# Attention stage of a streaming encoder: key pairs on column halves, one score burst per chunk, and a fixed TensorE order

## The chip, the core and the metric

The kernel is one launch on one core of a Trainium2 chip. The metric is the device time of one execution, in microseconds (us). A core has a tensor engine (PE, with its weight loads shown apart as PEld), a vector engine (DVE), a scalar engine (ACT), GpSimd (POOL) and a sync engine (SP). Each runs its own instruction stream in program order, and a DMA transfer is issued by one of these streams, here by SP and ACT. Matmul results land in PSUM, everything else lives in SBUF.

## The reference

The reference is one inference step of a small hybrid encoder: 2048 prompt tokens and 32 sample tokens, model width 1024. A gated delta-rule layer comes first, then one shared key/value projection, and then the layer that the change is about, sliding-window attention with learned sinks. Its core, shortened:

```python
CHUNK = 64; WINDOW_CHUNKS = 2; B_Q_HEADS = 16; B_KV_HEADS = 4; B_HD = 64

def sink_softmax(s, sinks):
    m = jnp.maximum(s.max(-1, keepdims=True), sinks)
    p = jnp.exp(s - m)
    return p / (p.sum(-1, keepdims=True) + jnp.exp(sinks - m))

# a chunk of 64 queries sees its own 64 keys and those of the two chunks before
s = jnp.einsum('bnqkgd,bnskd->bnkgqs', qb, kb)
o = jnp.einsum('bnkgqs,bnskd->bnqkgd', sink_softmax(s, sinks), vb)
out = (o * jax.nn.silu(z)) @ w_out
y = layer_norm(DN_ALPHA * x + out, ln_g, ln_b)
```

Chunk 0 sees one key chunk and chunk 1 two. The 32 sample tokens attend to 128 cached keys and 32 new ones. All is float32; the big products are done as three passes over a high and a low part of each operand, so that `out` is `g_hi*w_hi + g_hi*w_lo + g_lo*w_hi`.

## The kernel before

The stages run one after the other: projections of the first layer, the delta rule, its output projection and layer norm, then P2 (the query, gate, key and value projections of the second layer), then attention with its output projection. Only the end of P2 and the attention stage are touched.

**P2** (L1279 to L1281) is a list of products, each of 12 matmuls 128x416 in three passes. Its weights come through a ring of 12 tiles `w` of 512 KB, filled by DMAs that ACT issues (L1261). A generator (`late`) hands out the products, so that attention chunks can be set between the last of them.

**Attention** works in chunks of 64 queries, in the order 10 to 31, then 0 to 9. The first four chunks are set between the last P2 products; the rest come after P2. In a chunk there are two head sets (p = 0, 1) of eight heads. For each head set `chunk` does this:

- scores `S` (L1612): matmuls with 64 contraction rows, two of them on the two row halves of the array, into a PSUM tile; there are two `S` tiles after P2 is closed, one before
- softmax: the DVE's `reduce` of `S` for the negated maximum (L1487), a `min` with the sinks into `nm` (L1488), four exponentials on ACT (L1495), `es` (L1496 on DVE, L1497 on ACT), `sm` = sum plus `es` (L1498), its reciprocal (L1499)
- POOL scales the probabilities `P` by `sm` (L1620), in two instructions of 128x384
- six transposes of `P` into PSUM tiles `tr` (L1627), copied to `pt` by ACT (L1629) and by DVE (L1631)
- three value matmuls 128x256 (L1633), one for each key chunk, against `vd`, a block-diagonal 128x128 operand with 64 keys of one head in each diagonal block and zeros elsewhere; `graw` = result times gate, on DVE (L1636)

After two chunks a tile of 128 tokens is complete, and `finish` projects it: the load of `r` (the residual), `g_hi` on ACT (L1508), `g_lo` on POOL (L1509), then two column halves of 512. Each half is 24 matmuls 128x512 (L1520 to L1522) into one PSUM buffer `po`; there is only one such buffer, and the DVE's `r` <- `r`, `po` (L1523, a scalar_tensor_tensor) reads it out before the next half may start. Then come bn_stats (L1524), the layer-norm chain (L1526, POOL L466 and L468, L1530), ACT's scaling of `r` (L1531), and POOL's two passes over the 128x1024 tile, times `ln_g` (L1532) and plus `ln_b` (L1533), and the store of `y`.

The output weights (16 pieces of 512 KB) are loaded on SP after P2's tiles are given back (L999). The order of all engines' instructions in this stage is set by the scheduler of the framework from its own timing model; it puts `po` matmuls of an earlier tile between the steps of a chunk.

## Time and profile before

| what | value |
|---|---|
| median of 3 runs | 2208.47 us (2205.18 to 2213.85) |
| the profiled execution | 2207.43 us |
| its span | 2205.6 us |
| PE busy in the span | 2101.2 us, 95% |
| attention's first scores | 1781.56 us |
| last P2 matmul begins | 1794.63 us |
| last `po` matmul begins | 2195.75 us |

Times in the trace are counted from the start of the span. A timeline row has the start, the duration (both in us), the engine, the line, the operation with out<-in by the program's names, the count, and in brackets how long the engine had been idle and what released it. A group row has the count, the summed busy time and the mean in ns. A windows row has start and end, the length, then busy time and instruction count of PE, PEld, DVE, ACT and POOL, the clock that the tensor engine was granted (1.00 is full), the DMA share and GB/s. A matmul's duration is longer than its pace, since matmuls overlap in the pipeline; the pace is the distance of two starts.

### The profile page before, as it was taken

The page shows a single profiled execution, that of the slowest core. Times are in us where ns is not written, and L with a number is a line of the kernel's source. Part 1 is how long each engine was busy: PE and PEld are TensorE (multiplying, and loading weights), DVE is VectorE, ACT ScalarE, POOL GpSimd, SP SyncE. Part 2 cuts the span into 40 slices and gives each one's busy share as a digit, 9 for nine tenths or more (in the row PEclk, how much of TensorE's full clock was granted, in tenths as well). Part 3 has the DMA queues.
Part 4 walks back from the last instruction along what each step waited for, and adds up shares of the span by engine and source line. Part 5 has one row for each costly group of instructions (what it writes and reads, how often), then busy time and mean ns, then how long its engine had stood idle before and what let it go on. Part 6 is the DMA issues. An engine that isn't in the chain of part 4 may idle for free.

```text
span 2205.6 us, 37189 instructions
## 1 busy us (share of the span) xinstructions
PE 2101.2 (95%) x13370; PEld 1911.0 (87%) x13370; DVE 1486.4 (67%) x2771; ACT 912.1 (41%) x2405; POOL 713.6 (32%) x1176
## 2 busy tenths in 40 slices
PE   8999999999989999998888999899899988999997
PEld 6999999999979899887776888899899976888775
DVE  5889877776557589888865665555835566556663
ACT  5545545544412477677741111311311135444441
POOL 1212211161111288788841210000000025565663
PEclk9999999999999999999999999999999999999999
DMA  7756656567765635436737765888788895333321
GB/s 282 225 185 195 222 168 196 178 192 239 245 213 158 209 130 172 159 124 208 225 108 262 231 205 167 298 280 283 266 278 279 276 301 137 106 87 96 89 79 43
DMA packets 348377, 430.00 MB, mean 195 GB/s; under 512 B 78352, under 2 KB 276080, under 8 KB 348176
## 3 DMA queue, kind: packets, MB, share of 16 engines
q1 hardware_dynamic: 311280, 310.22, 44.3%
q10 hardware_dynamic: 36912, 117.40, 16.0%
q8 instruction: 106, 1.74, 0.3%
q14 instruction: 79, 0.65, 0.1%
HBM read 269.45 MB, written 158.44 MB: 194 GB/s over the span
## 4 chain that ended last, share of the span: by engine, by line
PE 69%; DVE 12%; POOL 5%; DMA 5%; ACT 4%; issue 3%; SPq 1%; ACTq 0%; DVEq 0%; POOLq 0%
PE ps L77 7%; PE ps L79 7%; PE ps L78 7%; PE ps L1279 5%; PE ps L1280 5%; PE ps L1281 5%; PE ot L1633 3%; PE po L1520 3%; PE po L1521 3%; PE S L1612 3%; PE po L1522 3%; PE po L1052 2%; PE po L1054 2%; PE po L1053 2%; PE tr L1627 2%
## 5 line engine op out<-in xcount | busy, mean ns | idle before, releaser
L77 PE MATMUL ps<-act_hi,w_hi 128*128 128x416 f32 x1280 | 457.2, 357 | 9.5 <-ACT w_hi L53 3.6
L79 PE MATMUL ps<-act_hi,w_lo 128*128 128x416 f32 x1280 | 449.5, 352 | 4.2 <-POOL w_lo L54 3.5
L78 PE MATMUL ps<-act_lo,w_hi 128*128 128x416 f32 x1280 | 450.0, 352 | 0.0
L77 PEld LDWEIGHTS ps<-act_hi,w_hi 128*128 128x128 f32 x1280 | 241.2, 188 | 13.7 <-ACT w_hi L53 4.2
L79 PEld LDWEIGHTS ps<-act_hi,w_lo 128*128 128x128 f32 x1280 | 241.2, 188 | 8.9 <-POOL w_lo L54 4.7
L78 PEld LDWEIGHTS ps<-act_lo,w_hi 128*128 128x128 f32 x1280 | 241.7, 189 | 2.7
L1279 PE MATMUL ps<-xs_h,w 128*128 128x416 f32 x560 | 200.0, 357 | 11.6 <-DVE ra L1336 7.6
L1280 PE MATMUL ps<-xs_l,w 128*128 128x416 f32 x560 | 200.3, 358 | 2.9 <-DVE xs_l L1182 2.9
L1281 PE MATMUL ps<-xs_h,w 128*128 128x416 f32 x560 | 198.9, 355 | 0.0
L54 POOL TENSOR_TENSOR w_lo<-w_raw,w_hi 128x1024 fp32r<-128x1024 f32 x32 | 81.0, 2530 | 357.6 <-ACT w_hi L53 343.6
L295 DVE SCALAR_TENSOR_TENSOR y<-R,convw,y 128x2083 f32<-128x2083 f32 (+2 forms) x78 | 175.3, 2247 | 24.4 <-ACT y L293 24.2
L585 POOL TENSOR_TENSOR tm<-L,Tt 128x60 f32<-128x60 f32 (+19 forms) x375 | 136.3, 363 | 87.2 <-PE sp L760 50.0
L588 POOL TENSOR_TENSOR Tt<-Tt,tm 128x60 f32<-128x60 f32 (+19 forms) x375 | 143.8, 383 | 28.3
L1620 POOL TENSOR_TENSOR P<-P,sm 128x384 f32<-128x384 f32 (+2 forms) x128 | 100.9, 810 | 120.4 <-DVE sm L1499 56.9
L1474 POOL MEMSET vd<- 64x768 f32 (+2 forms) x10 | 7.8, 779 | 398.2 <-DVE ra L1336 397.9
L1495 ACT ACTIVATE P<-S,nm 128x192 f32<-128x192 f32 (+2 forms) x260 | 104.8, 420 | 61.6 <-DVE nm L1488 49.0
L1279 PEld LDWEIGHTS ps<-xs_h,w 128*128 128x128 f32 x560 | 106.8, 191 | 14.6 <-DVE ra L1336 8.3
L1336 DVE SCALAR_TENSOR_TENSOR ra<-ps,u 128x416 f32<-128x416 f32 x60 | 35.4, 590 | 123.3 <-PE ps L1281 121.9
L1052 PE MATMUL po<-wo,g_hi 128*128 128x512 f32 (+1 forms) x272 | 111.0, 408 | 6.9 <-DVE r L1057 6.0
L1280 PEld LDWEIGHTS ps<-xs_l,w 128*128 128x128 f32 x560 | 106.5, 190 | 5.6 <-DVE xs_l L1182 4.2
L1281 PEld LDWEIGHTS ps<-xs_h,w 128*128 128x128 f32 x560 | 107.2, 191 | 1.3
L1054 PE MATMUL po<-wo,g_lo 128*128 128x512 f32 (+1 forms) x272 | 107.4, 395 | 0.0
(298 smaller groups left out, 4755.5 us busy)
## 6 DMA issues: line engine op xcount, KB each, us to landing
w<-s_w ACTq DMA_DIRECT2D x180, 512.0 KB, 4.7
s_w<-pre_hl SPq DMA_DIRECT2D x160, 256.0 KB, 2.5
w_raw<-in_w_in SPq DMA_DIRECT2D x32, 512.0 KB, 6.5
s_wo<-pre_hl SPq DMA_DIRECT2D x64, 256.0 KB, 4.0
gb<-s_gcum SPq DMA_DIRECT2D x34, 256.0 KB, 5.1
k<-s_k SPq DMA_DIRECT2D x34, 256.0 KB, 3.7
s_z<-z SPq DMA_DIRECT2D x40, 208.0 KB, 2.0
s_q<-y SPq DMA_DIRECT2D x8, 1024.0 KB, 5.2
```

The costliest lines, as they stand in the source:

```text
L77: nc.tensor.matmul(ps, hi[:, k, :], xh[:, k, :], start=(k == 0), stop=False)
L78: nc.tensor.matmul(ps, hi[:, k, :], xl[:, k, :], start=False, stop=False)
L79: nc.tensor.matmul(ps, lo[:, k, :], xh[:, k, :], start=False, stop=(k == KC - 1))
L295: self.nc.vector.scalar_tensor_tensor(out=y[:, a:z], in0=R[:, a + j:z + j], scalar=self.convw[:, i, j:j + 1], in1=y[:, a:z], op0=ALU.mult, ...
L585: P.tensor_tensor(out=tm[:n, i0 - k:, :w], in0=L[:n, i0:, j:j + 1].to_broadcast(sh), in1=Tt[:n, j:j + 1, :w].to_broadcast(sh), op=ALU.mult)
L588: P.tensor_tensor(out=Tt[:n, i0:, :w], in0=Tt[:n, i0:, :w], in1=tm[:n, i0 - k:, :w], op=ALU.subtract)
L1052: nc.tensor.matmul(ps[:n], ghi[:, k, :n], w[0][k][:, cs], start=(k == 0), stop=False)
L1054: nc.tensor.matmul(ps[:n], glo[:, k, :n], w[0][k][:, cs], start=False, stop=(k == KC - 1))
L1279: nc.tensor.matmul(ps, w[:, 0, k], xh[:], start=first and k == 0, stop=False, skip_group_check=True)
L1280: nc.tensor.matmul(ps, w[:, 0, k], xl[:], start=False, stop=False, skip_group_check=True)
L1281: nc.tensor.matmul(ps, w[:, 1, k], xh[:], start=False, stop=last and k == 3, skip_group_check=True)
L1495: nc.scalar.activation(P[u], src, AF.Exp, bias=nm[:, u:u + 1], scale=1.0, accum_out=sm[:, u:u + 1])
```

## The change

- **Values.** Two key chunks that begin at an even chunk form an aligned pair. Its 128 keys are one operand `vp` (new, 128x256 per pair, loaded by new DMAs beside `vd`). For a head set the pair is two matmuls with 64 output columns each, one on the lower and one on the upper column half (L1639), and the third key chunk two more, against 64 columns of `vd` (L1644). Four matmuls of 64x256 take the place of three of 128x256. `P` is laid out by head, and POOL scales the pair in one instruction (four times 128 wide, L1584) and the single chunk into a tile `P1` (L1588).
- **Scores.** Both head sets' scores are issued in one burst (L1565); the two softmaxes follow. The transposes and values of a chunk come one chunk later.
- **A fixed TensorE order.** The stage runs under a manual order for PE: scores of chunk n, six `po` matmuls, transposes of chunk n-1 (p = 0), six `po` matmuls, transposes (p = 1), six, values of chunk n-1, six. Three chunks (10, 11, 12) are set between the last P2 products by `alone`. The other engines' order is still the scheduler's. `finish` is a generator that gives six matmuls at a time, and `ready` issues the load of `r`, `g_hi` and `g_lo` of the next tile from the second half of a tile on.
- **Weights into the ring.** When P2's own weights have all been fetched, twelve pieces of the output weights are loaded into ring tiles by ACT's queue as these come free. The other four are loaded on SP after P2.
- The sample tokens move between chunk 31 and chunk 0, and the last tile's `y` is stored in two halves, on SP and on ACT.

How it moves instructions, at three places. First, PE where the first attention scores stand among P2's products. Before:

```order
L1281 MATMUL ps<-x_h,w 128x416
L1279 MATMUL ps<-x_h,w 128x416
L1612 MATMUL S<-kT,qs 128x192 x4
L1280 MATMUL ps<-x_l,w 128x416
L1281 MATMUL ps<-x_h,w 128x416
```

and now (the rows ahead of the scores belong to an earlier product, `xs_h`, those behind to the next one):

```order
L1284 MATMUL ps<-xs_h,w 128x416
L1285 MATMUL ps<-xs_l,w 128x416
L1286 MATMUL ps<-xs_h,w 128x416
L1565 MATMUL S<-kT,qs 128x192 x4
L1284 MATMUL ps<-x_h,w 128x416
```

Before, 56 matmuls of P2 are left behind the first scores; now 156 are.

Second, PE where one half of `po` ends and the next begins, in the steady part. Before, values, transposes and scores of one head set stand between pieces of a half; the last rows of a half and what follows are:

```order
L1522 MATMUL po<-wo,g_lo 128x512
L1633 MATMUL ot<-pt,vd 128x256
L1627 MATMUL tr<-ident,P 128x128 x2
L1633 MATMUL ot<-pt,vd 128x256 x2
L1627 MATMUL tr<-ident,P 128x128 x4
L1612 MATMUL S<-kT,qs 128x192 x4
L1520 MATMUL po<-wo,g_hi 128x512
```

and now (`po<-wo` are the last two of the eight weight rows of a half, `po<-w` the first ones, out of the ring):

```order
L1565 MATMUL S<-kT,qs 128x192 x8
L1729 MATMUL po<-wo,g_hi 128x512
L1730 MATMUL po<-wo,g_hi 128x512
L1731 MATMUL po<-wo,g_lo 128x512
L1729 MATMUL po<-wo,g_hi 128x512
L1730 MATMUL po<-wo,g_hi 128x512
L1731 MATMUL po<-wo,g_lo 128x512
L1615 MATMUL tr<-ident,P 128x128 x4
L1615 MATMUL tr<-ident,P_19350 128x128 x2
L1729 MATMUL po<-w,g_hi 128x512
L1730 MATMUL po<-w,g_hi 128x512
```

A half now always ends in the six matmuls behind the scores, and six transposes are all that stands between it and the next half.

Third, DVE around the read-out of `po` in the steady part. Before:

```order
L1487 TENSOR_REDUCE nm<-S 128x4
L1498 TENSOR_TENSOR sm<-sm,es 128x4
L1488 TENSOR_TENSOR nm<-nm,nsk 128x4
L1499 RECIPROCAL sm<-sm 128x4
L1496 TENSOR_TENSOR es<-nm,nsk 128x4
L1523 SCALAR_TENSOR_TENSOR r<-r,po 128x512
```

and now:

```order
L1498 TENSOR_REDUCE nm<-S 128x4
L1499 TENSOR_TENSOR nm<-nm,nsk 128x4
L1504 TENSOR_TENSOR es<-nm,nsk 128x4
L1498 TENSOR_REDUCE nm<-S 128x4
L1499 TENSOR_TENSOR nm<-nm,nsk 128x4
L1504 TENSOR_TENSOR es<-nm,nsk 128x4
L1734 SCALAR_TENSOR_TENSOR r<-r,po 128x512
L1506 TENSOR_TENSOR sm<-sm,es 128x4
L1617 COPY pt<-tr 128x384
L1735 BN_STATS st<-r 128x6
```

The read-out now stands behind the maxima of both head sets of the chunk whose scores were just issued. The diff, cut to its core:

```diff
@@ P2
             if self.loads and len(self.held) < self.RING:
                 what, slot = self.loads.pop(0)
                 w = self.wp.tile([128, 2, 4, 128], F32R, tag="w", name="w")
+                if what is None:
+                    flat = w[:].rearrange("p s k c -> p s (k c)")
+                    self.nc.scalar.dma_start(flat.bitcast(F32), self.T["wo"][1][slot // 2, :, slot % 2])
+                    self.out.append(flat)
...
-        self.loads = [(u, s) for u in units for s in self.slots(u)]
+        self.loads = [(u, s) for u in units for s in self.slots(u)] + [(None, i) for i in range(self.RING)]
@@ Attention
+        self.vp = one.tile([128, 16, 256], F32, tag="vp", name="vp")
...
+        both = T["bv"][a * 64:z * 64, :].rearrange("(c k) d -> k c d", k=128)
+        nc.sync.dma_start(self.vp[:, a // 2:z // 2, :], both)
...
+    def scores(self, n, ps=(0, 1)):
...
+                if pair is not None:
+                    part = flat[:, :, at:at + 128]
+                    nc.gpsimd.tensor_tensor(out=part, in0=part, in1=sm[:].unsqueeze(2).to_broadcast([128, 4, 128]),
+                                            op=ALU.mult)
+                if single is not None:
+                    f = sm[:].rearrange("r (h u) -> r h u", u=2).unsqueeze(3).to_broadcast([128, 2, 2, 64])
+                    nc.gpsimd.tensor_tensor(out=one[:].rearrange("r u h k -> r h u k"), in0=P[:, :, :, off:off + 64],
+                                            in1=f, op=ALU.mult)
...
+                if pair is not None:
+                    for h in range(2):
+                        hs = slice(h * 64, h * 64 + 64)
+                        nc.tensor.matmul(ot[hs, p], self.vp[:, pair, p * 128 + h * 64:p * 128 + h * 64 + 64],
+                                         pt[:, 2 * h:2 * h + 2, :], start=True, stop=one is None)
+                if one is not None:
+                    for h in range(2):
+                        hs = slice(h * 64, h * 64 + 64)
+                        nc.tensor.matmul(ot[hs, p], self.vd[:, one, p, hs], pt[:, 4:6, :],
+                                         start=pair is None, stop=True)
...
+    def alone(self, n):
+
+        self.scores(n, (0,))
+        for f in self.left_over[:1]:
+            f()
+        yield
+        for f in self.left_over[1:]:
+            f()
+        yield
+        self.scores(n, (1,))
+        self.turn(n, 0)
+        yield
+        self.left_over = [lambda: self.turn(n, 1), lambda: self.values(n)]
+        yield
+
+    def beside(self, n):
+
+        self.scores(n)
+        next(self.out)
+        for f in self.left_over:
+            f()
+            next(self.out)
+        self.left_over = [lambda: self.turn(n, 0), lambda: self.turn(n, 1), lambda: self.values(n)]
...
+            for j in self.finish(*got, last):
+                if j >= 4 and ahead is None and self.pend:
+                    ahead = self.ready()
+                yield
...
                 nc.tensor.matmul(ps[:n], glo[:, k, :n], w[0][k][:, cs], start=False, stop=(k == KC - 1))
+                if k % 2 == 1 and k < KC - 1:
+                    yield 4 * c + k // 2
             V.scalar_tensor_tensor(out=r[:n, cs], in0=r[:n, cs], scalar=ALPHA, in1=ps[:n], op0=ALU.mult, op1=ALU.add)
             V.bn_stats(out=st[:n, c, :], in_=r[:n, cs])
+            if c == 0:
+                yield 3
@@ program
-    order = list(range(10, 32)) + list(range(10))
...
+    order = list(range(10, 32)) + ["s"] + list(range(10))
+    with tc.manual_schedule(engines={ET.PE}):
+        drain(itertools.islice(late, 2))
+        for i in range(3):
+            for _ in att.alone(order.pop(0)):
+                drain(itertools.islice(late, 1))
+            att.load_kv(*((14, 18), (18, 24), (24, 32))[i])
+        drain(late)
+        p2.rest()
+        right.close()
+        att.open_right(right, p2.out)
+        att.load_kv(0, 8)
+        for n in order:
+            att.beside(n)
+        att.rest()
```

More of the change, by code (lines that the diff above doesn't have):

```diff
@@ L1460, in open_right @@
         self.ps_s.append(new_pool(tc, right, "u_ps", 1, PSUM, side=R))
-        rest = load_out_weights(self.nc, self.oone, self.T["wo"][1], self.nc.sync)
-        self.w = next(rest)
-        drain(rest)
-    def tables(self):
-        self.tabs = ln_tables(self.nc, self.oone, self.I["b_ln_g"], self.I["b_ln_b"])
+        have = len(pieces)
+        rest = self.oone.tile([128, 2 * KC - have, D], F32R, tag="wo", name="wo")
+        for i in range(have, 2 * KC):
+            nc.sync.dma_start(rest[:, i - have].bitcast(F32), self.T["wo"][1][i // 2, :, i % 2])
+        w = pieces + [rest[:, i] for i in range(2 * KC - have)]
+        self.w = [w[0::2], w[1::2]]
+        self.tabs = ln_tables(nc, self.oone, self.I["b_ln_g"], self.I["b_ln_b"])
     def load_kv(self, a, z):
@@ new lines, in turn @@
+    def turn(self, n, p):
+        nc, V, thr, ident = self.nc, self.nc.vector, self.thr, self.G["ident"]
+        P = self.probs.pop((n, p))
+        pt = thr.tile([128, 6, 128], F32, tag="pt", name="pt")
+        if n == "s":
+            for half in range(2):
+                tr = self.ps_t.tile([128, 3, 128], F32, tag="tr", name="tr")
+                nc.tensor.transpose(tr[:, 0, :], P[:, half, 0:128], ident[:, :])
+                nc.tensor.transpose(tr[:32, 1, :], P[:, half, 128:160], ident[:, :])
+                nc.scalar.copy(pt[:, 2 * half, :], tr[:, 0, :])
+                V.tensor_copy(pt[:32, 2 * half + 1, :], tr[:32, 1, :])
+        else:
+            _, _, pair, at, one, _ = self.keys(n)
+            src, (P, single) = [], P
+            if pair is not None:
+                src += [(2 * h + u, P[:, h, u, at:at + 128]) for h in range(2) for u in range(2)]
+            if one is not None:
+                src += [(4 + u, single[:, u].rearrange("r h k -> r (h k)")) for u in range(2)]
+            for copy in (nc.scalar.copy, V.tensor_copy):
+                now, src = src[:3], src[3:]
+                if now:
+                    tr = self.ps_t.tile([128, 3, 128], F32, tag="tr", name="tr")
+                    for i, (_, a) in enumerate(now):
+                        nc.tensor.transpose(tr[:, i, :], a, ident[:, :])
+                    c = now[0][0]
+                    copy(pt[:, c:c + len(now), :], tr[:, :len(now), :])
+        self.turned[n, p] = pt
@@ L1504, in finish, with rest, ready @@
+    def rest(self):
+        for f in self.left_over:
+            f()
+            next(self.out)
+        self.late = True
+        drain(self.out)
+    def ready(self):
+        nc, pool = self.nc, self.otwo
+        t0, n, graw = self.pend.pop(0)
         r = pool.tile([128, D], F32, tag="r", name="r")
@@ L1585, in start @@
-    def start(self, n):
-        nc, T = self.nc, self.T
-        if n % 2 == 0:
-            qs = self.two.tile([128, 2, 8, 64], F32, tag="qs", name="qs")
-            zs = self.two.tile([128, 8, 128], F32, tag="zs", name="zs")
-            for i in range(2):
-                tk = (n + i) * 64
-                nc.sync.dma_start(qs[:, i], T["bq"][:, :, tk:tk + 64].rearrange("h p t -> p h t"))
-            nc.sync.dma_start(zs[:], T["bz"][:, :, n * 64:n * 64 + 128].rearrange("h p t -> p h t"))
-            graw = self.thr.tile([128, 8, 128], F32, tag="graw", name="graw", bufs=4)
-            self.data = qs, zs, graw
@@ L1640, in flush @@
-    def flush(self, keep):
-        while len(self.pend) > keep:
-            self.finish(*self.pend.pop(0), late=(keep == 0), tail=(keep == 0 and len(self.pend) == 0))
+                queue.dma_start(self.O["y"][t0:t0 + n, cs], r[:n, cs])
+        yield 7
 class Filler:
@@ L1758, in program @@
     att.load_kv(8, 14)
-    order = list(range(10, 32)) + list(range(10))
-    for i in range(4):
-        drain(itertools.islice(late, 4))
-        att.chunk(order.pop(0))
-        if i != 2:
-            att.load_kv(*{0: (14, 18), 1: (18, 24), 3: (24, 32)}[i])
-    drain(late)
-    p2.rest()
-    right.close()
-    att.open_right(right)
-    att.load_kv(0, 8)
-    for n in order:
-        att.chunk(n)
-        if n == 15:
-            att.tables()
-        if n == order[-1]:
-            att.flush(1)
-            att.pend.insert(0, None)
-            att.pend.pop(0)
-            att.sample()
-            att.pend.reverse()
-        if n % 2 == 1:
-            att.flush(3 if n < 24 and n > 9 else 2)
-    att.flush(0)
+    order = list(range(10, 32)) + ["s"] + list(range(10))
[13 more added lines that the diff above has]
+        att.rest()
     left.close()
     right.close()
+    ring.close()
 def make_consts(tc, I, pool):
```

247 lines of the change are left out of this document (139 added, 108 removed).

## The prediction

> **What bounds the kernel now.** I read the page first.
>
> ```profile
> span 2205.6 us, 37189 instructions
> PE 2101.2 (95%) x13370; PEld 1911.0 (87%) x13370; DVE 1486.4 (67%) x2771; ACT 912.1 (41%) x2405; POOL 713.6 (32%) x1176
> PE 69%; DVE 12%; POOL 5%; DMA 5%; ACT 4%; issue 3%; SPq 1%; ACTq 0%; DVEq 0%; POOLq 0%
> ```
>
> PE is the bound nearly everywhere, so removed PE work is worth its time, and each new PE wait costs its time. Outside attention nothing changes, so I cut the end of the span into stretches.
>
> ```profile
> 1797.00:1835.00 38.00, 26.88 (x165) 19.21 (x163) 23.12 (x57) 19.56 (x83) 12.09 (x16) 0.96 1.05 339
> 1855.00:1947.00 92.00, 92.00 (x513) 74.03 (x512) 52.73 (x136) 44.68 (x168) 57.07 (x52) 1.00 0.30 87
> 1947.00:2130.00 183.00, 182.55 (x991) 144.10 (x989) 115.55 (x266) 84.09 (x326) 109.81 (x102) 1.00 0.34 93
> 2172.00:2206.00 34.00, 22.76 (x96) 13.97 (x96) 9.89 (x18) 3.47 (x4) 15.71 (x12) 0.93 0.15 51
> ```
>
> From 1855 to 2130 PE is never idle. Only the join of P2 and attention (1797 to 1835) leaves 38.0 - 26.9 = 11 us idle. The steady chunk, in PE's timeline:
>
> ```profile
> 1883.67 0.92 PE L1612 MATMUL S<-kT,qs 64*128 64x192 f32 x8
> 1884.52 0.50 PE L1520 MATMUL po<-wo,g_hi 128*128 128x512 f32 x1
> 1884.85 0.39 PE L1521 MATMUL po<-wo,g_hi 128*128 128x512 f32 x1
> 1885.08 0.40 PE L1522 MATMUL po<-wo,g_lo 128*128 128x512 f32 x1
> 1887.61 1.46 PE L1633 MATMUL ot<-pt,vd 128*128 128x256 f32 x6
> 1888.90 0.82 PE L1627 MATMUL tr<-ident,P 128*128 128x128 f32 x6
> 1889.65 0.92 PE L1612 MATMUL S<-kT,qs 64*128 64x192 f32 x8
> 1895.18 0.92 PE L1612 MATMUL S<-kT,qs 64*128 64x192 f32 x8
> ```
>
> A chunk lasts 1895.18 - 1883.67 = 11.51. The pace is 0.23 for a `po` matmul, 0.34 for the first after other work, 1.29 / 6 = 0.215 for a value pass, 0.65 to 0.75 for six transposes, 0.85 for eight score rows.
>
> **The work removed.** Twelve value passes a chunk (two for each fp32 matmul) become 16, in pairs on the two column halves. No row shows column halves. Row halves are shown: eight score rows of 192 columns take 0.85, where eight full rows in turn, at the value pace of 0.215 for 256 columns, would take 1.3. Bounds: side by side eight pass times, 8 x 0.215 = 1.72, 0.86 less than now; one after the other 16, 3.44, 0.86 more. I take side by side, because the rows of the same array in halves do it. [...] One burst of scores saves one entry, about 0.1. Per chunk 0.95, so 10.55 to 10.6 us, and over 31 chunks 29 to 30 us. The POOL pieces, the copies and the loads of `vp` have slack in the rows above: POOL is busy 57 of 92 us, DMA 0.30.
>
> PE's sum starts where the new order puts the first scores (1762.7) and ends with the last `po` matmul:
>
> ```profile
> 1762.68 0.36 PE L1280 MATMUL ps<-xs_l,w 128*128 128x416 f32 x1
> 1762.88 0.35 PE L1281 MATMUL ps<-xs_h,w 128*128 128x416 f32 x1
> 2195.75 0.40 PE L1522 MATMUL S<-wo,g_lo 128*128 128x512 f32 x1
> ```
>
> Work by pace and count: 156 P2 matmuls at 0.19, 30; 816 `po` at 0.23, 187; 372 value passes, 80; 64 score bursts at 1.06 with their entries, 68; transposes 40; sample and rest 6: 411 us. Before took 433 for it, so it lost 22 (11 idle above, the rest half clock and short waits). After, the work is 381.5; with the 9.8 us behind the last matmul as now, a kernel without waits ends at 1762.7 + 381.5 + 9.8 = 2154.
>
> **First wait: the queries.** In the new order the first scores are the next PE instruction when P2 has 156 matmuls left, and `qs` stands behind `kT`, `vp` and `vd` on SP.
>
> ```profile
> 1770.25 0.39 SPq L1470 DMA_DIRECT2D kT<-s_bk  x1
> 1774.08 1.42 SPq L1593 DMA_DIRECT2D qs<-s_bq  x2
> L1612 PEldq EVENT_SEMAPHORE  x1: 51/51/51, 1778.1 to 1778.1; - x1
> ```
>
> Before, the weight queue's wait for the scores' operands (last row, its answer for the tile `qs`) ended at 1778.1, hidden by P2; PE took them up at 1781.6. The SP instructions ahead of it are the same, plus one `vp` issue (about 0.5), less the stored `a` that stood at 1773.47. So PE sits from 1762.7 to about 1779.5, **17 us**, and 3 more at half clock. Bounds: 12, if SP comes free sooner with DVE less busy, to 20. The rest of the join: the 100 matmuls that used to run there run later, around the three chunks; there I allow 4 us for softmax waits and the four late weight pieces, where before lost 11.
>
> **Second wait: the one `po` buffer.** O1, the six matmuls behind the scores, ends a half in every chunk; six transposes later the next half wants the same buffer, and the DVE reads it out only after both maxima. Take T as the start of the scores. PE: scores 1.5, O1 0.34 + 5 x 0.23 to T+3.0, transposes to T+3.64; then it needs the buffer. DVE, by the one place where before had two maxima in a row:
>
> ```profile
> 1827.47 0.92 PE L1612 MATMUL S<-kT,qs 64*128 64x192 f32 x8
> 1828.44 0.96 DVE L1487 TENSOR_REDUCE nm<-S 128x4 f32<-128x768 f32 x1 [0.43 <-PE S L1612]
> 1829.43 0.16 DVE L1488 TENSOR_TENSOR nm<-nm,nsk 128x4 f32<-128x4 f32 x1
> 1829.71 0.95 DVE L1487 TENSOR_REDUCE nm<-S 128x4 f32<-128x768 f32 x1
> 1830.89 0.16 DVE L1496 TENSOR_TENSOR es<-nm,nsk 128x4 f32<-128x4 f32 x1
> 1893.34 0.69 DVE L1523 SCALAR_TENSOR_TENSOR r<-r,po 128x512 f32<-128x512 f32 x1 [0.40 <-PE po L1522]
> ```
>
> The chain ends 1831.05 - 1827.47 = 3.58 after the scores begin; with 0.69 for the read-out the buffer is free at T+4.25, so PE waits 0.6 in each chunk. But the small DVE steps are not always 0.16:
>
> ```profile
> 2051.90 1.18 POOL L1620 TENSOR_TENSOR P<-P,sm 128x256 f32<-128x256 f32 x2
> 2052.47 0.63 DVE L1488 TENSOR_TENSOR nm<-nm,nsk 128x4 f32<-128x4 f32 x1
> 2053.04 2.42 POOL L1533 TENSOR_TENSOR r<-r,ln_b 128x1024 f32<-128x1024 f32 x1
> 2053.13 2.36 DVE L1496 TENSOR_TENSOR es<-nm,nsk 128x4 f32<-128x4 f32 x1
> L1488 DVE TENSOR_TENSOR nm<-nm,nsk 128x4 f32<-128x4 f32 x46 | 14.0, 304 | 0.4
> L1509 POOL TENSOR_TENSOR g_lo<-graw,g_hi 128x1024 fp32r<-128x1024 f32 x12 | 28.7, 2388 | 3.8 <-ACT g_hi L1508 3.8
> L1508 ACT CAST g_hi<-graw 128x1024 fp32r<-128x1024 f32 x12 | 12.7, 1060 | 1.2 <-DVE graw L1636 1.2
> ```
>
> `nm` and `es` that begin during a POOL pass end with it. Before, nothing on PE's path stood behind them; now the read-out does. POOL has three passes of 2.4 us per tile. `g_lo` follows the values of an odd chunk and `g_hi` (1.06 on ACT), so it runs to about T+2.5 in one chunk of each two: `nm` ends 2.5 instead of 2.1, the second maximum 3.6, the read-out 4.7: PE waits **1.1**. In the other chunk `r` times `ln_g`, behind ACT's scaling, runs about T+0.4 to 2.75, and plus `ln_b` to 5.15: `nm` ends with the first and `es` with the second; then come the second maximum with its two small steps (1.35, to 6.5) and the read-out, to 7.2. PE waits **3.6**, up to 4.2 if the passes start 0.6 later. That is 4.7 for two chunks, 5.6 where chunks 2 to 9 put all three passes in a row: 13 tiles, 62 + 3, and 3 around the sample. **68 us**.
>
> **The clock after such a wait.** The granted clock in three gaps of PE and after:
>
> ```profile
> 1831.48 0.92 PE L1612 MATMUL S<-kT,qs 64*128 64x192 f32 x8 [2.44 <-ACT P L1495]
> 715.10:718.50 3.40, 0.00 (x0) 0.03 (x1) 1.92 (x5) 0.00 (x0) 0.00 (x0) 1.00 1.03 301
> 719.20:722.20 3.00, 2.41 (x9) 1.97 (x10) 0.00 (x0) 0.00 (x0) 0.00 (x0) 0.56 1.01 384
> 626.10:629.70 3.60, 0.05 (x2) 0.03 (x1) 2.39 (x4) 1.53 (x3) 0.00 (x0) 1.00 0.17 64
> 631.00:637.00 6.00, 4.84 (x19) 4.18 (x20) 3.87 (x7) 2.20 (x9) 1.10 (x1) 0.50 0.71 219
> 1832.50:1839.00 6.50, 5.95 (x25) 4.20 (x26) 5.16 (x11) 5.47 (x20) 6.10 (x6) 0.50 1.23 256
> ```
>
> A gap of 3.4 was followed by 3 us at half clock, one of 3.6 by over 6, and the one of 2.44 ahead of 1831.48 by 6.5. Half of such a time is lost, 1.6 to 3.3; none at least. For 13 gaps 0 to 43; I take 1.5 each, **20 us**. [...]
>
> **Sum**: 2154 + 17 + 3 + 4 + 68 + 20 = 2266 us on the profiled scale, whose execution (2207.43) is 1 us under the median: **2266 us**, 2.6% slower.
>
> **Rivals.**
>
> 1. *The read-out is never held by POOL's passes.* If POOL's passes fall elsewhere in the cycle (POOL has room: 57 of 92 us), or `nm` and `es` slip in between them, each of 29 chunks waits 0.6: 2154 + 24 + 17 = **2195**, 0.5% faster, at the bound. For it: POOL's passes wait for ACT and DVE, whose order I timed only by hand. Against: `nm` at 304 ns in the mean, twice its 160, shows that meetings are common already.
> 2. *The read-out comes in time.* The mechanism is the gain of the change with no wait at `po`: DVE reaches the read-out by T+2.95, so that the buffer is free when PE gets to it at T+3.64. Place: L1729 behind the first transposes; price: none; it decides once the chain from the scores is 0.6 shorter than the 3.58 of the rows (scores of the first head set done early, small steps back to back) and POOL keeps out of it. Then 2154 + 24 = **2178**, 1.3% faster. Against: both conditions have to hold, and the rows have neither.
> 3. *Column halves run one after the other*: 31 chunks x 1.72 = 53 more, **2319** with the waits, or 2248 under rival 1. For it: no row shows them. Decides from the first steady chunk. Against: the row halves.
> 4. *The queries come in time* (if SP is well ahead of PE): 20 less, 2246; this moves the size only.
>
> **How the numbers follow.** Chances: the forecast, with its size open, 0.58; rival 1 0.16; rival 2 0.13; rival 3 0.07; something unnamed 0.06. The forecast's own range is from 2154 + 12 + 4 + 50 + 0 = 2220 to 2154 + 27 + 75 + 43 = 2299. To hold 8 in 10 over the cases it goes from 2174, just under rival 2, to 2296. A measurement tells about 0.5% from no change, 2197 to 2220. Faster: rival 2, two thirds of rival 1, half of the unnamed: 0.27. Same: the rest of rival 1 and the low edge of the forecast: 0.10. Slower: 0.63.
>
> **What would show it.** The scores L1565 would start 17 us after their place in PE's stream, released by `qs`. The steady chunk would alternate between about 11.7 and 14 to 16 us, with PE's `po` L1729 idle on DVE `r` L1734; `nm` and `es` (L1499, L1504) would show means far over 160 ns, each long one ending with a POOL L1693, L1745 or L1746. Value passes would run with starts in pairs a few ns apart. It would be wrong if PE's idle time before L1729 is below 20 us in all, if the clock row stays at 9 there, or if the value rows come 0.215 apart.

## The result, and the profile after

The changed kernel takes 2314.12 us (median of four runs, 2311.99 to 2317.93); the kernel before, beside it, 2211.16. The ratio is 1.0475, with a 95% interval of 1.0453 to 1.0496: 4.75% slower. The prediction said slower, with 2266 us and a range to 2296; it had the direction and about half of the size.

The page of the changed kernel:

```profile
span 2313.7 us, 37336 instructions
PE 2115.7 (91%) x13494; PEld 1894.0 (82%) x13494; DVE 1497.1 (65%) x2769; ACT 913.6 (39%) x2405; POOL 711.8 (31%) x1172
```

PE's share falls from 95% to 91%. PE's waits from 1755 us on (what waited, what for, us in total, times, longest):

```profile
PE po L1729 <- DVE r L1734: 38.2, 20, 4.5
PE ot L1639 <- DVE graw L1648: 22.1, 31, 3.6
PE S L1565 <- DMA qs<-s_bq: 15.9, 1, 15.9
PE S L1565 <- ACT vb L1408: 11.5, 1, 11.5
PE po L1729 <- DVE sm L1506: 7.8, 9, 0.9
PE tr L1615 <- POOL P L1584: 4.6, 2, 3.8
```

The `po` waits are here (38.2, 7.8 and some small ones, 48.0 in all), and so is the wait for `qs`. The second row was in no sum: the values wait for `graw` in every chunk. The windows view shows the clock that PE was granted over whole stretches with such waits (the number after POOL's count):

```profile
1762.00:1797.00 35.00, 15.96 (x86) 13.66 (x84) 13.03 (x34) 4.94 (x20) 9.14 (x12) 0.74 1.02 266
1797.00:1866.00 69.00, 45.34 (x230) 37.49 (x231) 22.07 (x60) 18.21 (x70) 11.52 (x13) 0.77 0.76 217
1866.00:2120.00 254.00, 218.10 (x1271) 156.27 (x1270) 134.11 (x312) 99.93 (x379) 128.09 (x120) 0.96 0.27 74
2160.00:2306.00 146.00, 120.62 (x633) 83.87 (x631) 71.03 (x142) 46.55 (x160) 69.86 (x61) 0.91 0.19 56
```

Two chunks of the steady part in PE's timeline:

```profile
1991.35 0.65 PE L1639 MATMUL ot<-pt,vp 128*64 128x256 f32 x4
1991.83 0.60 PE L1644 MATMUL ot<-pt,vd 128*64 128x256 f32 x4
1993.05 0.65 PE L1639 MATMUL ot<-pt,vp 128*64 128x256 f32 x4 [0.62 <-DVE graw L1648]
1994.07 0.51 PE L1729 MATMUL po<-w,g_hi 128*128 128x512 f32 x1
1995.66 1.57 PE L1565 MATMUL S<-kT,qs 64*128 64x192 f32 x16
2000.33 0.47 PE L1729 MATMUL po<-w,g_hi 128*128 128x512 f32 x1 [0.87 <-DVE sm L1506]
2008.24 1.57 PE L1565 MATMUL S<-kT,qs 64*128 64x192 f32 x16
2014.03 0.50 PE L1729 MATMUL po<-w,g_hi 128*128 128x512 f32 x1 [1.96 <-DVE r L1734]
```

The first of the two lasts 2008.24 - 1995.66 = 12.58 us, against 11.51 before. It holds a `po` wait of 0.87 and a values wait of 0.62; without them it would be 11.09, where the forecast had 10.55 to 10.6. The second has a `po` wait of 1.96, and at 2014.6 the clock drops to half for 3.4 us. Such chunks last 15.3 to 15.4, and 13.75 where the clock stays. In chunks 3, 5, 7 and 9 the long wait is 4.0 to 4.5 us, and chunks 3, 5 and 7 last 18 us. What holds the read-out there, in the timeline's rows of POOL, DVE and PE in chunk 5:

```profile
2197.12 2.37 POOL L1693 TENSOR_TENSOR g_lo<-graw,g_hi 128x1024 fp32r<-128x1024 f32 x1
2197.93 1.59 DVE L1499 TENSOR_TENSOR nm<-nm,nsk 128x4 f32<-128x4 f32 x1
2199.46 2.33 POOL L1746 TENSOR_TENSOR r<-r,ln_b 32x1024 f32<-32x1024 f32 x1
2199.55 2.27 DVE L1504 TENSOR_TENSOR es<-nm,nsk 128x4 f32<-128x4 f32 x1
2203.03 0.69 DVE L1734 SCALAR_TENSOR_TENSOR r<-r,po 128x512 f32<-128x512 f32 x1
2203.77 0.79 PE L1729 MATMUL po<-w,g_hi 128*128 128x512 f32 x1 [4.00 <-DVE r L1734]
```

`nm` ends with `g_lo` and `es` with the pass of `ln_b`, as the prediction described it for the other chunk of each two.

The sum of the prediction against the trace, from 1762.6 us to the end. PE's gaps over 0.1 us are added up by what follows them; the loss to the clock is half of PE's busy time in the half-clock spells (15 spells, 99 us, 64 of them busy).

| term | predicted | measured |
|---|---|---|
| PE's work | 381.5 | 400.1 |
| wait for the queries | 17 | 15.9 |
| other waits, 26.2 of them at the join | 4 | 28.1 |
| waits at the `po` buffer | 68 | 48.0 |
| second head set's values | 0 | 18.5 |
| half clock | 3 + 20 | 32.1 |
| behind the last matmul | 9.8 | 8.4 |
| end of the span, with 1762.6 | 2266 | 2313.7 |

For the kernel before, the count has to start at the same place in the program. "The change" and the prediction put 156 P2 matmuls behind the first scores; the trace of the changed kernel has 168. Before, the last 168 begin at 1760.4 us, and from there its trace has 418.6 us of work and 16.8 lost; the changed kernel, from 1763.4, has 399.4 of work. So the change saves 19 us of PE work, not 29.5, and adds 126 us of waits and half clock.

### The profile page after: what moved, and what is told of

It reads as the page before. It is cut to its first block, busy times and chain, and to the rows that moved or that the text cites. A ratio compares the mean times of both kernels' runs of the same rounds, so it can differ in the third digit from the quotient of the medians.

```text
span 2313.7 us, 37336 instructions
## 1 busy us (share of the span) xinstructions
PE 2115.7 (91%) x13494; PEld 1894.0 (82%) x13494; DVE 1497.1 (65%) x2769; ACT 913.6 (39%) x2405; POOL 711.8 (31%) x1172
## 4 chain that ended last, share of the span: by engine, by line
PE 63%; DVE 17%; DMA 6%; POOL 5%; issue 3%; ACT 3%; SPq 1%; ACTq 0%; DVEq 0%; POOLq 0%
PE ps L77 7%; PE ps L79 7%; PE ps L78 7%; PE ps L1284 5%; PE ps L1285 5%; PE ps L1286 5%; PE po L1729 3%; PE po L1052 2%; PE po L1731 2%; PE po L1054 2%; PE po L1053 2%; PE po L1730 2%; DVE nm L1498 2%; POOL Tt L588 2%; PE ot L1639 2%
## 5 line engine op out<-in xcount | busy, mean ns | idle before, releaser
L1729 PE MATMUL po<-w,g_hi 128*128 128x512 f32 (+1 forms) x192 | 91.6, 477 | 48.0 <-DVE r L1734 38.2
L1584 POOL TENSOR_TENSOR P<-P,sm 128x512 f32<-128x512 f32 x62 | 64.5, 1041 | 191.1 <-DVE sm L1507 124.6
L1284 PEld LDWEIGHTS ps<-xs_h,w 128*128 128x128 f32 x560 | 106.4, 190 | 14.1 <-DVE ra L1341 7.9
L1498 DVE TENSOR_REDUCE nm<-S 128x4 f32<-128x768 f32 (+3 forms) x66 | 60.2, 914 | 87.7 <-PE S L1565 86.1
```

Of the source, the lines that this page charges most:

```text
L1284: nc.tensor.matmul(ps, w[:, 0, k], xh[:], start=first and k == 0, stop=False, skip_group_check=True)
L1498: V.tensor_reduce(out=nm[:, :nsub], in_=S, axis=AX.X, op=ALU.max, negate=True)
L1729: nc.tensor.matmul(ps[:n], ghi[:, k, :n], w[0][k][:, cs], start=(k == 0), stop=False)
```

## Experiments: the waits of the steady chunk

**The place where a half ends.** One line gives one more slot of six `po` matmuls ahead of chunk 13, so that each half lies within one chunk.

```diff
+        next(att.out)
         for n in order:
             att.beside(n)
```

> The changed kernel with one more slot of six po matmuls ahead of chunk 13, so that a half of po ends in the last slot of a chunk (in front of the scores) and the next half begins behind them. Theory (the wait at the one po buffer comes from the place of the half's end): the 48 us of PE idle in front of L1729 fall below 6, the half-clock spells of the steady part go with them (about 20 us of lost work), 2314 - 48 - 20 = about 2246. Rival (DVE is late in any case, and the wait only moves to the transposes or the values): total PE idle stays within 15 us of the changed kernel's 110 and the time over 2295.

Measured: 2270.82 us, ratio 1.0294 (1.0264 to 1.0324). Between 1870 and 2100 us no wait at L1729 is left, and all that PE waits for is

```profile
PE ot L1639 <- DVE graw L1648: 15.0, 19, 1.0
PE po L1731 <- POOL g_lo L1693: 2.7, 9, 0.3
```

The half-clock loss falls from 32.1 to 13.6 us. So the wait and most of the half clock came from the place of the half's end. It brings 43 us and not 68: the transposes wait 8 us more than in the changed kernel, the `g_lo` matmuls 5 and the values 2, and the half clock gives 18.5 us, not 20. At the join 12.4 us of wait for `g_hi` appear where 11.5 for `vb` had been. The profiled execution also reached attention 4.5 us later than that of the changed kernel, which is no effect of the edit.

**POOL's passes.** In this run the two passes over `r` are left out, so that its layer norm lacks its gain and offset for all tiles but the last.

```diff
-            nc.gpsimd.tensor_tensor(out=r[:n], in0=r[:n], in1=tabs[0][:n], op=ALU.mult)
-            nc.gpsimd.tensor_tensor(out=r[:n], in0=r[:n], in1=tabs[1][:n], op=ALU.add)
```

> The changed kernel without POOL's two passes over r (times ln_g, plus ln_b) for all tiles but the last: this part of the layer norm is left out. Theory (nm and es that meet a POOL pass end with it, and the read-out of po stands behind them): nm L1499 falls from a mean of 569 ns to under 300, the po waits of 2 and 4 us become waits of 0.6 to 0.9 as in the other chunks, 48 us become about 25, the half-clock spells behind them go: about 2270. Rival (the long waits come from the order on DVE or from ACT alone): waits of 2 and 4 us stay, over 2300.

Measured: 2267.27 us, ratio 1.0278 (1.025 to 1.0306). PE's waits in the steady part, and the group of `nm`:

```profile
PE po L1729 <- DVE sm L1506: 7.8, 9, 0.9
PE po L1729 <- DVE r L1734: 4.2, 9, 0.5
L1499 DVE TENSOR_TENSOR nm<-nm,nsk 128x4 f32<-128x4 f32 x38 | 10.6, 279 | 1.3
```

The long waits are gone; the steady chunks last 12.2 and 12.6 us; the half-clock loss is 10.7. The 0.9 that stays stands in the chunks where `g_lo` is still there. The long waits did come from POOL's passes.

**What it is in these steps that waits.** The passes stay; instead, the maximum, a second copy of `nm` and the sink's exponential go through spare columns of the scores' PSUM tile, so that no small step reads two operands from SBUF.

```diff
-        V.tensor_reduce(out=nm[:, :nsub], in_=S, axis=AX.X, op=ALU.max, negate=True)
-        V.tensor_tensor(out=nm[:, :nsub], in0=nm[:, :nsub], in1=nskc, op=ALU.min)
+        m, m2, e = (raw[:, i // 2, i % 2, 192:192 + nsub] for i in range(3))
+        V.tensor_reduce(out=m, in_=S, axis=AX.X, op=ALU.max, negate=True)
+        V.tensor_tensor(out=nm[:, :nsub], in0=m, in1=nskc, op=ALU.min)
+        V.tensor_tensor(out=m2, in0=m, in1=nskc, op=ALU.min)
...
-        V.tensor_tensor(out=es_[:, :nsub], in0=nm[:, :nsub], in1=nskc, op=ALU.subtract)
-        nc.scalar.activation(es_[:, :nsub], es_[:, :nsub], AF.Exp)
-        V.tensor_tensor(out=sm[:, :nsub], in0=sm[:, :nsub], in1=es_[:, :nsub], op=ALU.add)
+        V.tensor_tensor(out=m2, in0=m2, in1=nskc, op=ALU.subtract)
+        nc.scalar.activation(e, m2, AF.Exp)
+        V.tensor_tensor(out=sm[:, :nsub], in0=e, in1=sm[:, :nsub], op=ALU.add)
```

> The changed kernel with the softmax's small DVE steps rewritten so that each has only one operand in SBUF: the maximum, its second copy and the exponential of the sink go through spare columns of the scores' PSUM tile (one small step more per head set). POOL's passes stay where they are. Theory (a DVE step with two SBUF operands waits for a POOL pass, one with a single SBUF operand doesn't): the means of these steps fall to under 250 ns, the po waits of 2 and 4 us become about 1.2 (0.87 and the added step), 48 us become 30 to 35, the half-clock spells behind them go, about 2275. Rival (DVE is held back by POOL's work whatever its operands, or the long waits come from ACT): the steps stay long, within 10 us of 2314.

Measured: 2257.2 us, ratio 1.0219 (1.0202 to 1.0236), 57 us better than the changed kernel. The groups of these steps (`nm` is now L1500, the subtraction L1505, the sum L1507):

```profile
L1505 DVE TENSOR_TENSOR S<-S,nsk 128x4 f32<-128x4 f32 x40 | 6.8, 170 | 15.3 <-ACT P L1504 12.9
L1500 DVE TENSOR_TENSOR nm<-S,nsk 128x4 f32<-128x4 f32 x40 | 6.5, 162 | 1.4
L1507 DVE TENSOR_TENSOR sm<-S,sm 128x4 f32<-128x4 f32 x40 | 6.3, 160 | 0.2 <-ACT S L1506 0.2
```

From a mean of 569 ns for `nm` to 162, with all of POOL's passes in place. Counted in the trace: in the changed kernel 60 of these small steps begin inside a POOL instruction, 57 of them end within 0.05 us of it, and the longest takes 2.29 us; here 100 begin inside one, and the longest takes 0.171. So in these two traces it is the steps with two SBUF operands that are held to the end of a POOL instruction, and the same steps with one are not. The `po` waits fall to 8.3 us, below the 30 to 35 expected, because the new dependencies also let the scheduler put the subtraction behind the read-out; that part of the gain belongs to the order.

**Values of the second head set.** Two ways to take their wait away: apart in time, and apart in PSUM.

```diff
# apart in time
-        self.left_over = [lambda: self.turn(n, 0), lambda: self.turn(n, 1), lambda: self.values(n)]
+        self.left_over = [lambda: self.turn(n, 0), lambda: (self.turn(n, 1), self.values(n, (0,))),
+                          lambda: self.values(n, (1,))]
# apart in PSUM
-        ot = self.ps_o.tile([128, 2, 256], F32, tag="ot", name="ot")
+        ots = [self.ps_o.tile([128, 2, 256], F32, tag="ot", name="ot")[:, 0],
+               self.ps_t.tile([128, 3, 128], F32, tag="tr", name="ot1")[:, 0:2].rearrange("q u k -> q (u k)")]
```

> The changed kernel with the values of the two head sets in two places: those of p = 0 directly behind the second transposes, those of p = 1 where both stood, six po matmuls apart. Theory (0.62 us in each chunk are a wait of the second head set's values for the DVE's graw of the first, since both lie in one PSUM tile): the 31 waits of 0.62 in front of L1639 vanish, 19 us, less about 5 for one more change of tile shape in a chunk: 2295 to 2300. Rival (the array drains there for another reason, such as the start of a new accumulation): the gap moves with the values and the time stays at 2314.

> The changed kernel with the second head set's values in a PSUM tile of its own (a bank of the transposes' pool), everything in the old place. Theory (the second head set waits for the DVE's graw of the first because both share one tile): the waits of 0.62 in front of L1639 go, 31 x 0.62 = 19 us, with no new change of tile shape: about 2295. Rival (the array itself pauses between two accumulations on column halves): gap and time stay, 2314.

Measured: 2304.5 us (ratio 1.0448, 1.0418 to 1.0478) and 2289.2 (1.0367, 1.0332 to 1.0402). In both the waits for `graw` are gone from the steady part. With a PSUM tile of its own the second set's values follow the first's without a gap and the shorter chunk lasts 11.75 us in place of 12.58; with the values apart it lasts 12.1, 0.35 more, about what a second block of values pays for its own change of tile shape in and out (0.35 by the rows of the next section). The array did not pause by itself here: what PE waited for, 0.62 us a chunk, was the DVE's read of a tile that both head sets shared. That the two do not touch the same bytes of it did not help. The new tile also comes from another PSUM pool, so this run does not tell whether the tile or its place in PSUM counts.

## Experiments: what column halves are worth

**At the same order.** The changed kernel with the old values (block-diagonal `vd`, three matmuls 128x256).

```diff
-                        nc.tensor.matmul(ot[hs, p], self.vp[:, pair, p * 128 + h * 64:p * 128 + h * 64 + 64],
-                                         pt[:, 2 * h:2 * h + 2, :], start=True, stop=one is None)
...
+                for j in range(nj):
+                    nc.tensor.matmul(ot[:, p], self.vd[:, kc0 + j, p, :], pt[:, 2 * j:2 * j + 2, :],
+                                     start=(j == 0), stop=(j == nj - 1))
```

> The changed kernel with the old values (three matmuls 128x256 against block-diagonal vd, the old layout of P and two POOL instructions of 384), the new order kept. It tells what the column halves are worth where the order is the same. Theory (side by side, but with an entry and an exit of about 0.1 each for the change of tile shape): 12 passes at 0.215 are 2.58, the halves take about 2.06; the values cost 0.5 more in 31 chunks, 16 us, 2330. Rival A (the full 0.86 of the prediction): 2341. Rival B (the halves gain nothing): within 5 us of 2314.

Measured: 2315.43 us, ratio 1.049 (1.0465 to 1.0516). By the time alone, rival B holds. The trace says why the time misleads. A block of values here, and what follows it:

```profile
1974.93 1.46 PE L1630 MATMUL ot<-pt,vd 128*128 128x256 f32 x6
1977.00 1.53 PE L1630 MATMUL ot<-pt,vd 128*128 128x256 f32 x6 [0.61 <-DVE nb L1729]
1978.18 0.58 PE L1715 MATMUL po<-w,g_hi 128*128 128x512 f32 x1
```

The block takes 1978.18 - 1974.93 = 3.25 us; in the changed kernel 1994.07 - 1991.35 = 2.72, both with the wait of 0.6. The halves save 0.53 us a chunk, 16 us over 31, as the theory had it. But in this run PE's waits and half clock are 16 us less (gaps 106.6 for 110.5, half clock 19.8 for 32.1): the long chunks last 13.9 us, with no half clock behind a wait of 1.65 (behind the one that ends at 1958.06 the `po` matmuls keep their pace of 0.23). What the values gained, the waits gave back, and a time alone would have called it nothing. PE's work in this run is 416.4 us: of the 19 that the change saves, the halves bring 17, and the fixed order with its single score burst 2.

That the halves save 0.53 and not 0.86 shows at the two ends of a block. In the changed kernel the step from the last `po` matmul to the first pair takes 0.33, the next pair 0.27, the step back 0.31 and the first `po` matmul 0.34. With full tiles these four take 0.23, 0.215, and 0.45 for the last two together. That is 0.35 more in a chunk, close to the 0.33 that is missing.

**In the old order.** The kernel before with key pairs on column halves, and nothing else.

```diff
+            if pair is not None:
+                for h in range(2):
+                    hs = slice(h * 64, h * 64 + 64)
+                    nc.tensor.matmul(ot[hs, p], self.vp[:, pair, p * 128 + h * 64:p * 128 + h * 64 + 64],
+                                     pt[:, 2 * h:2 * h + 2, :], start=True, stop=single is None)
```

> The kernel before with one part of the change alone: key pairs on column halves (vp, the layout of P, the two POOL instructions), with the old order. Theory (halves run side by side, 12 passes become 8 pass times): 0.86 us in each of 31 chunks off a stage that PE bounds, 27 us, about 2182. Rival (the changes of tile shape eat it, or the halves are paid for in entries): within 0.5% of 2208.

Measured: 2224.03 us, ratio 1.01 (1.0056 to 1.0145): slower by 1%, which neither the theory nor the rival had, with hardly more PE waits than before (16.0 us for 13.7). PE's timeline shows where it goes:

```profile
1897.91 0.40 PE L1520 MATMUL po<-wo,g_hi 128*128 128x512 f32 x1
1898.24 0.65 PE L1647 MATMUL ot<-pt,vp 128*64 128x256 f32 x2
1898.82 0.50 PE L1521 MATMUL po<-wo,g_hi 128*128 128x512 f32 x1
1899.16 0.39 PE L1522 MATMUL po<-wo,g_lo 128*128 128x512 f32 x1
1899.48 0.43 PE L1647 MATMUL ot<-pt,vp 128*64 128x256 f32 x1
1900.49 0.55 PE L1641 MATMUL tr<-ident,P 128*128 128x128 f32 x3
```

The scheduler sets `po` matmuls into this head set. The row at 1898.24 is the two passes of one column half, 0.27 apart: the matmul of the other half stands behind the `po` matmuls, so nothing runs beside them. The two parts take 0.58 and 1.01 to the start of what follows, 1.59 in all, where the six full passes took 1.29 in one go. The trace has 25 of the 60 head sets with a pair and a single chunk split like this; most of the other 35 take 1.02 in one go. Between 1870 and 2100 us the tile shape changes 184 times, before 84 times. A step from a `po` matmul to a value pass takes 0.33 and back 0.31, where the pace is 0.23 and 0.21: 0.1 for each change, before what the second step of either loses. Added up over the stage, the value passes take 85 us in both kernels, so that the unsplit head sets gain what the split ones lose, and the matmuls around them take 14 us more, 2 of them half clock. So a change of tile shape cost time here, and these rows give its price; what the array does in that time they do not show.

## Experiments: the join, and the parts together

The wait of 11.5 us for `vb` begins on SP. ACT's row, and the two of SP ahead of it:

```profile
1857.13 0.26 ACT L1408 COPY vb<-ps 32x128 f32<-32x128 f32 x1 [10.66 <-DMA s_bv<-va]
1844.36 1.97 SPq L1472 DMA_DIRECT2D wo<-s_wo  x4
1846.42 1.25 SPq L1410 DMA_DIRECT2D s_bv<-va  x1
```

The four last pieces of the output weights, 2 MB, are issued ahead of the store of `va`, whose buffer `vb` wants. That these pieces are what makes the store late is read from this order; no run issued them elsewhere with the rest as it was. The next run gives `vb` other buffers, and loads `kT` and `qs` first:

```diff
-            vb = self.wk.tile([128, TB], F32, tag="rs", name="vb")
+            vb = self.wk.tile([128, TB], F32, tag="ra", name="vb", bufs=4)
...
+        nc.sync.dma_start(self.kT[:, :, 512:896], self.T["bk"][:, :, 512:896].rearrange("a p t -> p a t"))
+        self.start(10)
         for i in range(2):
             nc.sync.dma_start(self.nsk[i * 64:i * 64 + 64, :], I["sinks"][i].partition_broadcast(64))
```

> The changed kernel with two edits at the join of P2 and attention: kT and qs of the first chunks are issued ahead of the sinks, vp and vd, and the last part of the stored values has a buffer of its own, so that ACT does not wait for the store of the part before it. Theory: the first wait of 15.9 us falls to about 8, the wait of 11.5 us in front of chunk 13's scores to under 3, and some half clock goes with it: 2314 - 8 - 9 - 3 = about 2294. Rival (the transfers are what is late, in whatever order they are issued): the waits come back under other names, over 2306.

Measured: 2304.88 us, ratio 1.0442 (1.0415 to 1.0469). The first edit did its part, the second did not:

```profile
PE po L1732 <- ACT g_hi L1695: 11.7, 1, 11.7
PE S L1568 <- DMA qs<-s_bq: 9.0, 1, 9.0
```

The wait for `qs` falls from 15.9 to 9.0, though the next scores then wait 9.8 us for `P` where they waited 3.0. The other comes back in front of the first `po` matmul, where ACT now stands until the store of `vb` has landed:

```profile
1847.30 1.04 ACT L1695 CAST g_hi<-graw 128x1024 fp32r<-128x1024 f32 x1 [5.89 <-DMA s_bv<-vb]
```

`g_hi` lies in memory that P2 gives back; that this is the link was read from the code and the releaser, not tried.

Then the parts were put together. In the first combination the scheduler sets chunks 10 to 13 between P2's products as in the kernel before; from chunk 14 on the fixed order holds, each half of `po` lies within a chunk, the second head set's values have a tile of their own, and `vb` has the buffers of the run before.

```diff
-            for _ in att.alone(order.pop(0)):
-                drain(itertools.islice(late, 1))
+        drain(itertools.islice(late, 4))
+        n = order.pop(0)
+        for p in range(2):
+            att.scores(n, (p,))
+            att.turn(n, p)
+        att.values(n)
...
+        att.left_over = [lambda: None] * 3
         for n in order:
             att.beside(n)
```

> The parts together, to see whether the changed order can pay: chunks 10 to 13 set between P2 products by the scheduler as before the change, then the fixed order from chunk 14 on with halves of po that begin behind the scores, the second head set's values in a tile of their own, and the buffer of its own for the stored values. Theory: the steady chunk falls from 14 to about 11.2 (11.5 before), the join costs about what it cost before: 2195 to 2215, within 0.5% of 2208 or just faster. Rival (the order's other waits, on g_lo and P, remain): over 2225.

Measured: 2237.84 us, ratio 1.0141 (1.0116 to 1.0166). The rival holds; PE's longest item between 1860 and 2130 us is new:

```profile
PE tr L1615 <- ACT pt L1617: 19.2, 18, 1.9
```

The transposes wait for ACT's copy of the first half, which stands behind exponentials that wait for `nm`. So the second combination takes the small steps through PSUM.

> The combination run before (chunks 10 to 13 by the scheduler, halves of po beginning behind the scores, values of the second head set in a tile of their own) with the same small DVE steps through PSUM. Theory (its waits for ACT's pt copy of up to 1.9 us come from exponentials that are late because nm was held by POOL): the 22 us of waits of L1615 for pt fall under 10, 2238 becomes about 2220, still not faster than 2208. Rival (ACT's own order sets the copy): 2235 or more.

Measured: 2210.7 us, ratio 1.0006 (0.9991 to 1.0022), no difference from before and 10 us better than the theory. That wait is down to

```profile
PE tr L1616 <- ACT pt L1618: 1.8, 8, 0.2
```

and the steady chunks last 10.67 and 11.40 us in turn, 11.03 in the mean for 11.51. What is left lies at the join: 7.2 us of wait for an activation of ACT, which stands over the issue of ring loads, and 10.2 for the single scores tile, which is held until `sm`.

```diff
# third combination
-            if self.loads and len(self.held) < self.RING:
+            if self.loads and len(self.held) < self.RING - (self.LAG if self.loads[0][0] is None else 0):
...
-    RING = 12
+    RING, LAG = 12, 3
# fourth
-    RING, LAG = 12, 3
+    RING, LAG = 12, 7
```

> The second combination with its join mended: the output weights go into ring tiles only three loads behind P2's own (the last three and the other four pieces on SP), so that ACT is less often held by an issue that waits for a free tile; the first four chunks keep the old small steps, so that the single scores tile comes free sooner; their values follow each head set; qs of chunk 14 is loaded ahead of the last pieces. Theory: of the 17 us in front of L1284 and the scores of chunks 10 to 13 some 12 go, and 4 of half clock: 2211 - 15 = about 2195, faster than before by about 0.6%. Rival (the extra loads at the join keep the transfers late, whoever issues them): 2205 to 2215, no difference from before.

> The third combination with one number changed: the output weights follow P2's own loads by seven ring tiles, not three, so that ACT issues five pieces and SP seven more into the ring. In the run before, ACT stood 16.7 us over the issue of five pieces, and PE waited 8.85 us for the activation behind it. Theory (the issue waits for a ring tile that is still in use): the wait in front of L1292 falls under 2 us and 2 to 4 us of half clock go: 2203 - 10 = about 2193, 0.7% faster than before. Rival (the pieces that SP now loads later are missed at the first po matmuls): what is won in front of L1292 is lost in front of L1752, 2200 to 2206.

Measured: 2203.34 us (ratio 0.9975, 0.9961 to 0.9989) with three, 2196.68 (0.996, 0.9948 to 0.9973) with seven. The third lies between its theory and its rival, the fourth near its theory. With three, one row of ACT stands behind a PE wait of 8.85 us; ahead of it is ACT's row of five issues, and the last two rows are pieces of the chain of releases that leads there (start, length, what was waited for):

```profile
1777.80 15.86 ACTq L1270 DMA_DIRECT2D w<-s_wo  x5
1793.71 0.52 ACT L1331 ACTIVATE a<-ps 128x416 f32<-128x416 f32 x1 [16.73 <-DMA w<-s_wo]
1777.80 8.38 DMA w<-s_wo
1786.25 7.02 DMA w<-s_wo
```

The expectations put this down to ring tiles still in use. The trace does not show that: each of the five issues begins within 0.1 us of the landing of an earlier transfer (the second, at 1782.24, behind a landing at 1782.16; the last, at 1793.34, behind one at 1793.27), and none begins behind a PE matmul.

With seven, PE's waits have it at

```profile
PE ps L1292 <- ACT a L1331: 2.2, 1, 2.2
```

The page of the fourth combination:

```profile
span 2192.0 us, 37366 instructions
PE 2082.7 (95%) x13494; PEld 1871.2 (85%) x13494; DVE 1459.8 (67%) x2827; ACT 905.5 (41%) x2405; POOL 714.3 (33%) x1172
```

The third and this one are the only versions that are faster than the kernel before, by 0.25% and 0.4%. PE's busy time is 18.5 us under before's; waits and half clock behind 1762.6 us are 28 us, where before had 17 and the changed kernel 143.

## Why the prediction was half right

The direction held. The size failed in three steps: a wait that the prediction put at nothing (the values of the second head set, 18.5 us), an allowance for the join that came from no row (4 us, measured 26), and the gain of the column halves (26.7 us, measured 17).

**Right.** PE bounds the stage, and the change trades work for waits. The wait for the queries was 15.9 for 17. The `po` buffer waits in every chunk, because a half ends six transposes ahead of the next and the read-out stands behind two maxima; undoing the place, the passes or the second SBUF operand each took more than half of it away. Half clock followed the longer waits: six of the eight of 1.95 to 2.06 us. The first two rivals, no hold by POOL and no wait at `po`, are out.

**The values, "0.86 less than now".** The halves do run side by side: the four rows of `vp` at 1991.35 begin in pairs, 7 ns apart in a pair, and 0.48 us later `vd` follows. The term left out the change of tile shape, 0.35 a chunk at the two ends of a block, and its sum per chunk, 0.95, came out at 0.42 (11.51 to 11.09). The two runs on the values give 0.53 for the halves at one order and a loss of 0.5 a chunk in another. The work saved is 19 us where 29.5 were forecast, 10 us short. Rival 3 named 2319 us, near the measured time, but for halves in turn, which they are not; that it is near is luck.

**A wait that was in no term.** The prediction asked who reads `po`, and not who reads `ot`. Before, transposes, scores and `po` matmuls lay between the values of the two head sets; in the new order they are neighbours, and the DVE's `graw` of the first stands between them: 0.62 in 30 chunks, 18.5 us; a tile of its own took 25 us off the time.

**The join, "I allow 4 us".** Measured 26.2. 11.5 are the wait for a store issued behind two megabytes of weights, 10.4 more the waits of 3.0 to 3.8 us between scores, `P` and values of chunks 10 to 12, which share one scores tile and have little P2 work between them. The step that failed is the allowance itself: it came from no row, where before's own 11 us were the nearest bound, and even these would have been too few.

**The `po` wait, 68 us.** Measured 48.0. The wait of 3.6 in one of two chunks was 1.95 to 2.06 in chunks 16 to 30, because the passes start earlier than T+0.4: `ln_g` at 2007.02 and `ln_b` at 2009.48 against scores at 2008.24, so that only `nm` meets one. In chunks 3, 5, 7 and 9 it was 4.0 to 4.5, as `nm` and `es` both did. That this term was 20 us too high made the miss in the total smaller, which is luck too.

**The clock, 23 us.** Measured 32.1: right in kind. Waits of 1.95 to 2.06 us were enough in six of eight chunks. All 15 spells up to the last matmul begin on one grid of 3.41 us and last whole multiples of it, from 3.41 (2014.61 to 2018.03, for one) to 17.07 (1765.44 to 1782.51). Laid over PE's idle time, the grid sorts the waits. In the changed kernel's trace from 1762 us on, PE was idle for at least 1.95 us in every one of the 15 grid windows that ended in a drop of the clock, and for at most 1.68 in each of the 115 other windows at full clock. The two waits of 2.00 and 1.97 us that no drop followed are cut in two by a grid line (at 1987.3 and 2069.2 us), with 1.59 and 1.36 in the larger parts.

The range ended at 2296 because its upper end had nothing for the wait at `ot` and at most 4 us for the join beside the queries, where 18.5 and 26 were measured.

## What to carry to other kernels

When a scheduler's order is replaced by a fixed one, list for each PSUM tile who must read it before PE's next write, and put PE work at least as long as the whole chain to that read in between; do this for every shared tile, not only the one that the change is about. Small DVE steps with two SBUF operands ended here with the GpSimd pass that they met (57 of 60 in the changed kernel, the longest after 2.29 us), and with one they took at most 0.171, so keep them off the path, or let one operand come from PSUM. Column halves paid here only in unbroken blocks: a chunk's block lost about 0.35 us at its ends, and a half whose partner stood elsewhere ran alone, its two passes 0.27 apart.

## What the runs showed of the hardware that was not expected

- PE gaps of 1.95 to 2.06 us were followed by half clock in six of eight chunks (3.4 us from 2014.6 on, for one), while the gap of 1.65 us with the old values that ends at 1958.06 was not. The idle time within one window of a 3.41 us grid tells them apart: from 1762 us on, 1.95 us or more ahead of each of the changed kernel's 15 drops and 1.68 or less in its 115 other windows at full clock; in the kernel before, 2.44 ahead of the one drop and 1.30 or less in the 123 others. It is not that clear in the earlier stages, where three drops of the changed kernel follow windows with 1.15 to 1.39 us of idle time (from 809.7, 837.0 and 1140.8 us).
- Taking one SBUF operand away from the 128x4 steps shortened them from up to 2.29 us to at most 0.171 (`nm` from 569 ns to 162, in the mean of the steady part), with the GpSimd passes unmoved.
- A change between full tiles and column halves cost about 0.1 us on the first step each way, and 0.35 us in all for a block of a chunk's values. In the old order, 100 more changes in 230 us and halves parted from their partners turned a saving of passes into a loss of 1%.
- In the third combination ACT stood 16.7 us over the issue of five loads, each of which began behind the landing of an earlier transfer, and PE waited 8.85 us for the activation behind them.
